# Moving the stationary operands of a two-layer decoder trunk to multiples of 512 bytes in SBUF

## The chip, the cores and the metric

The kernel runs on one core of one Trainium2 chip. The metric is the device time of one execution in microseconds (us). TensorE (PE in the profile) multiplies: it loads a stationary operand of up to 128 columns (LDWEIGHTS, shown as PEld) and then streams a moving operand of up to 512 columns past it. VectorE (DVE), ScalarE (ACT) and GpSimd (POOL) work on SBUF; SyncE (SP) issues the DMAs.

## The reference

Two layers over x (256 tokens, 1024 wide), all in float32:

```python
h = rmsnorm(x, g_mix);  proj = h @ w_in            # 1024 -> 7244 columns
A = stick_breaking_attention(qa, ka, va)           # 8 heads of 64
B = forgetting_attention(qb, kb, vb, log_f)        # 8 heads of 64
C = indexed_sparse_attention(qc, kc, vc, ...)      # top 64 keys, 2 kv heads
y = sum_b sigmoid(gate_b) * (branch_b @ w_branch[b])
x = x + y @ w_out
x = x + relu(rmsnorm(x, g_mlp) @ w_up)**2 @ w_down # 1024 -> 4096 -> 1024
```

After both layers a last RMSNorm with g_final gives the output. The weights are 149 MB, each read once.

## The kernel before, in words

Every product is made of three: both operands are split into a high part (float32r) and a rest, and `mm3` (L124 to L128) multiplies high by high (L126), high by low and low by high (L127, L128). Weights come by DMA on SP's queue into `raw` (four buffers); ACT makes the high part `whi` (L92), DVE the rest `wlo` (L93), four buffers each.

A matmul is written `pe.matmul(out, stationary, moving)`. The profile and the order of instructions write it the other way round, out<-moving,stationary: `mm<-whi,uh 128x512` streams 512 columns of `whi` past a stationary block of 128 columns of `uh`, and `mm<-xTh,whi 128x256` streams the 256 tokens of `xTh` past a stationary block of `whi`.

Products come in two manners. With weights stationary and 256 tokens moving: the q and k projections (`feat`), the gates, the branches (moving operand `k2h`, `k2l`) and w_up. With activations stationary and up to 512 weight columns moving (`stream_groups` and `stream_tok`, L198 to L219): the columns of attention C, the values (stationary `xTh`, `xTl`), w_out (stationary `yT`) and w_down (stationary `uh`, `ul`). In w_down the stationary operand changes with every matmul except between L126 and L127, which share `uh`.

Attention goes by pairs of heads. q is stationary (`qs`), k moves (L351, L352); the probabilities are transposed by TensorE, where the probabilities `e` or `R` are stationary and `ident` moves (L442); then v (`v` or `vc`) is stationary and the transposed probabilities `pTh`, `pTl` move (L458). Stick-breaking attention (L609 to L630) does the following for each of its four pairs of heads in each layer: ACT writes `th` = tanh(z/2) (L615), POOL masks it in place (two AFFINE_SELECTs, L618) and makes `m` = 0.5 - 0.5 th (L620), DVE runs a scan over `m` backwards (L626) and multiplies by 1 + th (L627). The scan takes `m` one element late, so `m` has 769 elements and three memsets:

```python
m = work.tile([128, 769], F32, name="m", tag="w3", bufs=4)
pool.tensor_scalar(m[:, 0:768], th..., -0.5, 0.5, ...)        # L620
pool.memset(m2[:, :, 0:1], 0.0)                               # L622
pool.memset(m2[:, :, 128:129], 0.0)                           # L623
pool.memset(m[:, 768:769], 0.0)                               # L624
dve.tensor_tensor_scan(R[:, ::-1], m[:, 1:769][:, ::-1], ...) # L626
```

SBUF is given out by pools that lie behind one another: `const`, `wp` (raw, whi, wlo), `t2` (xTh, xTl), `small`, and behind `small` either the layer's attention pool or, in the same place, its MLP pool (`uh`, `ul`). Within a pool tiles follow one another, each rounded up to 32 bytes; tiles of one tag share buffers of the largest one's size. So the size of every tile sets where those behind it lie. The order of work on each engine is set by a scheduler when the program is built.

Of the kernel before, what the change touches and what calls it, by code (L numbers as in the profile page):

```python
# [9 lines left out]
F32 = mybir.dt.float32  # L10
# [3 lines left out]
OP = mybir.AluOpType  # L14

T, D, DEPTH, COLS, DFF = 256, 1024, 2, 7244, 4096
NH, DH, BW, TOPK = 8, 64, 512, 64
FL0 = 3072
C0, CN = 3072, 1100
# [8 lines left out]
def AP(src, off, dims):  # L28
    return bass.AP(tensor=src.tensor, offset=src.offset + off, ap=[list(d) for d in dims])
# [3 lines left out]
def trunk_kernel(ctx: ExitStack, tc: tile.TileContext, x, positions, g_mix, w_in, b_forget, w_branch,  # L33
                 w_out, g_mlp, w_up, w_down, g_final, out):
    nc = tc.nc
    act, dve, pool, pe, dma = nc.scalar, nc.vector, nc.gpsimd, nc.tensor, nc.sync

    const = ctx.enter_context(tc.tile_pool(name="const", bufs=1))
    wp = ctx.enter_context(tc.tile_pool(name="wp", bufs=3))
    tp2 = ctx.enter_context(tc.tile_pool(name="t2", bufs=1))  # L40
    small = ctx.enter_context(tc.tile_pool(name="small", bufs=4))
# [5 lines left out]
    def at_tile(name="at"):  # L47
        return ps.tile([128, 512], F32, name=name, tag="at", bufs=2)
# [7 lines left out]

    xh = [const.tile([128, 2, 512], F32, name=f"x{h}") for h in range(2)]
    xs = [[xh[h][:, j, :] for h in range(2)] for j in range(2)]
    gload = const.tile([16, 128], F32, name="gload")
    gload2 = const.tile([16, 128], F32, name="gload2")  # L60

    def load_x(h):
        dma.dma_start(xh[h], AP(x, h * 512, [[D, 128], [128 * D, 2], [1, 512]]))
# [72 lines left out]
    def blk(tiles, k, c0=0, c1=256, p0=0, p1=128):  # L136
        h, l = tiles[k // 2]
        return h[p0:p1, k % 2, c0:c1], l[p0:p1, k % 2, c0:c1]
# [82 lines left out]
    att = None  # L221
    for layer in range(DEPTH):
# [8 lines left out]
        with tc.tile_pool(name=f"att{layer}", bufs=1, reuse_waits="tile") as att:  # L231
            work = att

            rp = at_tile("rp")
            for j in range(2):
                pe.transpose(rp[:, j * 128:j * 128 + 128], rstd[:, j:j + 1].to_broadcast([128, 128]), ident)
            rb = small.tile([128, 256], F32, name="rb", tag="rb", bufs=1)
            act.activation(rb, rp[:, 0:256], AF.Copy)


            ct = att.tile([128, 2, CN], F32, name="ct", tag="G", bufs=1)
            def ct_done(c0, n, o):
                for j in range(2):
                    act.activation(ct[:, j, c0:c0 + n], o[j][:, :n], AF.Copy, scale=rstd[:, j:j + 1])
# [4 lines left out]
            ct_done(368, 368, stream_tok(xt, 8, w_in, wi0 + C0 + 368, COLS, 368))  # L249

            if layer == 0:
                dma.dma_start(gload2, AP(g_mlp, 0, [[128, 16], [1, 128]]))
                pos = const.tile([128, 2], I32, name="pos")
                dma.dma_start(pos, AP(positions, 0, [[1, 128], [128, 2]]))
# [14 lines left out]
                ends = const.tile([128, 768], mybir.dt.bfloat16, name="ends")  # L269
# [6 lines left out]
                for q in range(2):  # L276
                    dve.tensor_scalar(self_[32 * q:32 * q + 8, :], ident[32 * q:32 * q + 8, 32 * q:32 * q + 8], -1.0, None,
                                      op0=OP.mult)
# [60 lines left out]
            for n, c in enumerate((KI, KC, KC + 64)):  # L339
# [3 lines left out]
                p = at_tile("kT")  # L343
# [15 lines left out]
            for j, c, n in SEG:  # L359
                for h in range(4):  # L360
                    z = at_tile("zi")
                    i = h % 2
# [5 lines left out]
                                             op0=OP.mult, op1=OP.add)  # L368

            for j, c, n in SEG:  # L370
                s = sc[:, c:c + n]
# [47 lines left out]
            p = at_tile("cum")  # L419
# [10 lines left out]
            p = at_tile("cumt")  # L430
            pe.matmul(p[:, 0:8], tri[:, 0:128], lf[:, 0, 0:8], start=True, stop=True)
            pe.matmul(p[:, 8:16], tri[:, 128:256], lf[:, 0, 0:8], start=True, stop=False)
            pe.matmul(p[:, 8:16], tri[:, 0:128], lf[:, 1, 0:8], start=False, stop=True)
            ctok = att.tile([128, 2, NH], F32, name="ctok")
            dve.tensor_copy(ctok, p[:, 0:16].rearrange("p (j h) -> p j h", j=2))


            def p_parts(e, i, scale):

                p = pt_tile("pT")  # L440
                for q in range(3):
                    pe.transpose(p[:, q * 128:q * 128 + 128], e[:, i, q * 128:q * 128 + 128], ident)  # L442
                hi = work.tile([128, 384], F32R, name="pTh", tag="pTh", bufs=2)
                lo = work.tile([128, 384], F32R, name="pTl", tag="pTl", bufs=2)
                act.activation(hi, p[:, 0:384], AF.Copy, scale=scale)
                dve.scalar_tensor_tensor(lo, p[:, 0:384], scale, hi.bitcast(F32), op0=OP.mult, op1=OP.subtract)
                return hi, lo

            def av_pair(parts, vwin, dst):


                o = av_tile()
                for i in range(2):
                    c = i * 256
                    for s, a, b, c0 in ((0, 0, 256, 0), (1, 256, 384, 128)):
                        v = vwin(i, s)
                        for n, p in enumerate(parts[i]):
                            pe.matmul(o[:, c + c0:c + 256], v, p[:, a:b], start=s == 0 and n == 0,  # L458
                                      stop=s == 1 and n == 1)
                hi, lo = dst  # L460
                t = work.tile([128, 256], F32, name="avs", tag="avs", bufs=2)
                for i in range(2):
                    act.activation(t[half(i)], o[half(1 - i), i * 256:i * 256 + 256], AF.Copy)
                for i in range(2):
                    dve.tensor_add(t[half(i)], o[half(i), i * 256:i * 256 + 256], t[half(i)])
                act.activation(hi, t, AF.Copy)
                dve.tensor_sub(lo, t, hi.bitcast(F32))
# [58 lines left out]
            def qk(z, qs, ks, b, i, opened=False):  # L526
                q, (kt, lo) = qs[b // 2], ks[b // 2]
                for j, c, n in SEG:
                    qk2(z[:, c:c + n], q[:, b % 2, i, j * 128:j * 128 + 128], kt[:, b % 2, i, 0:n],
                        lo[:, b % 2, i, 0:n], not opened, j == 1 or not opened)  # L530
# [79 lines left out]
            for b in range(4):  # L610
                th = work.tile([128, 2, 384], F32, name="th", tag="w3", bufs=4)
                for i in range(2):
                    z = at_tile("za")
                    qk(z, qa, ka, b, i)
                    act.activation(th[:, i, :], z[:, 0:384], AF.Tanh, scale=0.5)  # L615
                for c in (0, 256):
                    v = th[:, :, c:c + 128]
                    pool.affine_select(v, v, [[0, 2], [-1, 128]], OP.is_gt, -1.0, base=0, channel_multiplier=1)  # L618
                m = work.tile([128, 769], F32, name="m", tag="w3", bufs=4)
                pool.tensor_scalar(m[:, 0:768], th.rearrange("p i s -> p (i s)"), -0.5, 0.5, op0=OP.mult, op1=OP.add)  # L620
                m2 = m[:, 0:768].rearrange("p (i s) -> p i s", i=2)
                pool.memset(m2[:, :, 0:1], 0.0)  # L622
                pool.memset(m2[:, :, 128:129], 0.0)  # L623
                pool.memset(m[:, 768:769], 0.0)  # L624
                R = work.tile([128, 768], F32, name="R", tag="w3", bufs=4)
                dve.tensor_tensor_scan(R[:, ::-1], m[:, 1:769][:, ::-1], ends[:, ::-1], 0.0, op0=OP.mult, op1=OP.add)  # L626
                dve.scalar_tensor_tensor(R, th.rearrange("p i s -> p (i s)"), 1.0, R, op0=OP.add, op1=OP.mult)  # L627
                Rv = R.rearrange("p (i s) -> p i s", i=2)
                parts = [p_parts(Rv, i, 0.5) for i in range(2)]
                av_pair(parts, lambda i, s: va[:, s, 2 * b + i, :], blk(brA, b))  # L630
# [124 lines left out]
```

## Time and profile before

| | |
|---|---|
| median of 3 runs | 902.84 us (901.21 to 903.78) |
| the profiled execution's own time | 900.61 us |
| span of the profiled execution, first to last instruction | 898.6 us |
| granted TensorE clock, mean | 0.997 |
| PE busy | 882.3 us (98%) |
| DVE, ACT, POOL busy | 640.2 us, 530.2 us, 115.2 us |

PE's busy time counts matmuls whose ends are modelled and overlap, so it does not tell how fast TensorE works. That is read from the starts: the distance between the starts of successive matmuls is what each of them costs the stream. The timeline prints the start of each.

### The profile page before, as it was taken

Reading aid. Unit: us, or ns where it says so; the run is one execution under the profiler, and the core shown is the slowest. Engines: PE = TensorE matmul, PEld = TensorE weight load, DVE = VectorE, ACT = ScalarE, POOL = GpSimd, SP = SyncE. Lnnn points to the kernel's source line nnn. Section 1 sums busy time; section 2 is a strip of 40 time slices with the busy share of each in tenths; the row PEclk is TensorE's granted clock in tenths of the full one; section 3 lists DMA queues with packets and bytes.
Section 4 is the critical chain, followed back from the end, with each engine's and each line's share of the span. In section 5 each row is a group of like instructions: output and inputs, shape, how many; then the busy total and the mean of one; then the engine's idle time right before and its main releaser. Section 6 shows DMA issues by size and latency. Waiting matters only on the chain.

```text
span 898.6 us, 15648 instructions
## 1 busy us (share of the span) xinstructions
PE 882.3 (98%) x6174; PEld 828.8 (92%) x6174; DVE 640.2 (71%) x1032; ACT 530.2 (59%) x874; POOL 115.2 (13%) x222
## 2 busy tenths in 40 slices
PE   7999999999999999999999999999999999999996
PEld 7999999999989999888899999999999999998884
DVE  6889878997766666445468998799967666664542
ACT  6766876785465555434366759587744665553432
POOL 2300403352000000000011004043500100000001
PEclk9999999999999999999999999999999999999998
DMA  8746454244565554555466373543455565555521
GB/s 299 232 141 188 146 172 152 95 141 144 186 188 188 186 182 176 185 187 172 143 195 213 114 225 104 168 158 95 141 187 179 174 195 185 185 187 187 187 94 47
DMA packets 114777, 151.08 MB, mean 168 GB/s; under 512 B 2928, under 2 KB 82832, under 8 KB 114704
## 3 DMA queue, kind: packets, MB, share of 16 engines
q1 hardware_dynamic: 114704, 150.08, 51.2%
q8 instruction: 49, 0.80, 0.3%
q14 instruction: 24, 0.20, 0.1%
HBM read 149.02 MB, written 1.05 MB: 167 GB/s over the span
## 4 chain that ended last, share of the span: by engine, by line
PE 91%; DVE 4%; POOL 2%; issue 2%; DMA 1%; SPq 0%; ACT 0%; POOLq 0%; DVEq 0%; ACTq 0%
PE mm L128 26%; PE mm L126 26%; PE mm L127 26%; PE av L458 2%; PE at L128 1%; PE at L127 1%; PE at L126 1%; PE pT L442 1%; DVE R L626 1%; POOL m L620 1%; PE xtp L175 1%; DVE ksl L160 1%; DMA x<-in_x_dram 1%; POOL th L618 1%; DVE wlo L93 1%
## 5 line engine op out<-in xcount | busy, mean ns | idle before, releaser
L93 DVE TENSOR_TENSOR wlo<-raw,whi 128x1024 fp32r<-128x1024 f32 (+3 forms) x289 | 349.8, 1213 | 192.5 <-ACT whi L92 191.4
L92 ACT ACTIVATE whi<-raw 128x1024 fp32r<-128x1024 f32 (+3 forms) x289 | 298.6, 1035 | 278.8 <-PE mm L127 142.2
L126 PE MATMUL mm<-xTh,whi 128*128 128x256 f32 x1136 | 322.7, 284 | 0.0
L128 PE MATMUL mm<-xTh,wlo 128*128 128x256 f32 x1136 | 322.2, 284 | 0.0
L127 PE MATMUL mm<-xTl,whi 128*128 128x256 f32 x1136 | 322.0, 283 | 0.0
L126 PEld LDWEIGHTS mm<-xTh,whi 128*128 128x128 f32 x1136 | 217.6, 192 | 0.3
L127 PEld LDWEIGHTS mm<-xTl,whi 128*128 128x128 f32 x1136 | 217.6, 192 | 0.2
L128 PEld LDWEIGHTS mm<-xTh,wlo 128*128 128x128 f32 x1136 | 217.6, 192 | 0.1
L128 PE MATMUL mm<-whi,ul 128*128 128x512 f32 x256 | 101.6, 397 | 0.0
L127 PE MATMUL mm<-wlo,uh 128*128 128x512 f32 x256 | 101.5, 396 | 0.0
L126 PE MATMUL mm<-whi,uh 128*128 128x512 f32 x256 | 101.1, 397 | 0.0
L192 POOL TENSOR_TENSOR ms<-ss 128x2 f32<-128x2 f32 (+1 forms) x6 | 4.3, 719 | 481.1 <-ACT junk L185 301.6
L128 PEld LDWEIGHTS mm<-whi,ul 128*128 128x128 f32 x256 | 48.2, 188 | 11.7
L127 PEld LDWEIGHTS mm<-wlo,uh 128*128 128x128 f32 x256 | 48.2, 188 | 11.6
L126 PEld LDWEIGHTS mm<-whi,uh 128*128 128x128 f32 x256 | 48.2, 188 | 11.6
L128 PE MATMUL mm<-k2h,wlo 128*128 128x256 f32 x192 | 54.1, 284 | 0.0
L126 PE MATMUL mm<-k2h,whi 128*128 128x256 f32 x192 | 53.6, 284 | 0.0
L127 PE MATMUL mm<-k2l,whi 128*128 128x256 f32 x192 | 53.6, 282 | 0.0
L127 PE MATMUL mm<-wlo,xTh 128*128 128x512 f32 (+2 forms) x128 | 46.3, 363 | 0.0
L126 PE MATMUL mm<-whi,xTh 128*128 128x512 f32 (+2 forms) x128 | 46.1, 365 | 0.1
L128 PE MATMUL mm<-whi,xTl 128*128 128x512 f32 (+2 forms) x128 | 45.7, 363 | 0.0
L491 POOL TENSOR_SCALAR e<-e,rs 128x128 f32<-128x128 f32 x64 | 34.4, 556 | 16.6 <-DVE rs L488 16.4
(214 smaller groups left out, 1306.4 us busy)
## 6 DMA issues: line engine op xcount, KB each, us to landing
raw<-in_w_in_dram SPq DMA_DIRECT2D x48, 1024.0 KB, 5.0
raw<-in_w_up_dram SPq DMA_DIRECT2D x32, 1024.0 KB, 5.3
raw<-in_w_down_dram SPq DMA_DIRECT2D x32, 1024.0 KB, 4.9
raw<-in_w_branch_dram SPq DMA_DIRECT2D x12, 1024.0 KB, 4.9
raw<-in_w_out_dram SPq DMA_DIRECT2D x8, 1024.0 KB, 5.0
raw<-in_w_in_dram SPq DMA_DIRECT2D x8, 736.0 KB, 5.8
raw<-in_w_in_dram SPq DMA_DIRECT2D x3, 728.0 KB, 4.4
out_dram<-x SPq DMA_DIRECT2D x4, 256.0 KB, 2.4
```

Source lines behind the costliest of these rows:

```text
L92: act.activation(h3[:, i:i + m], raw[:, i:i + m], AF.Copy)
L93: dve.tensor_sub(l3[:, i:i + m], raw[:, i:i + m], h3[:, i:i + m].bitcast(F32))
L126: pe.matmul(o, ah, bh, start=start, stop=False)
L127: pe.matmul(o, ah, bl, start=False, stop=False)
L128: pe.matmul(o, al, bh, start=False, stop=stop)
L160: dve.tensor_sub(lo[half(i), :, i, :], src[half(i)], dst[half(i), :, i, :].bitcast(F32))
L175: pe.transpose(p[:, i * 256 + j * 128:i * 256 + j * 128 + 128], xs[j][h][:, c:c + 128], ident)
L442: pe.transpose(p[:, q * 128:q * 128 + 128], e[:, i, q * 128:q * 128 + 128], ident)
L458: pe.matmul(o[:, c + c0:c + 256], v, p[:, a:b], start=s == 0 and n == 0, stop=s == 1 and n == 1)
L491: pool.tensor_scalar(e[:, i, c:c + n], e[:, i, c:c + n], rs[:, i, j:j + 1], 1.0, op0=OP.mult, op1=OP.mult)
L618: pool.affine_select(v, v, [[0, 2], [-1, 128]], OP.is_gt, -1.0, base=0, channel_multiplier=1)
L620: pool.tensor_scalar(m[:, 0:768], th.rearrange("p i s -> p (i s)"), -0.5, 0.5, op0=OP.mult, op1=OP.add)
```

## The change

Tiles get other sizes or other pools, so that the tiles behind them lie elsewhere: `gload2` takes the buffer of `gload` (512 bytes less in `const`), `rb` is padded from 256 to 280 floats and `ctok` (64 bytes) moves into `small` (160 bytes more there, so that the pools behind it start at byte 119,808, which is 234 times 512, where they started at 120,160); `ct` is padded from 1100 to 1152 columns; `m` shrinks from 769 to 768 elements, so that the buffers of its tag are 3072 bytes apart where they were 3104. For that `m` is written one element earlier from `th` taken one element later, which leaves out one of its three memsets.

```diff
-    gload = const.tile([16, 128], F32, name="gload")
-    gload2 = const.tile([16, 128], F32, name="gload2")
+    gload = const.tile([16, 128], F32, name="gload", tag="gload")
...
-            rb = small.tile([128, 256], F32, name="rb", tag="rb", bufs=1)
+            rb = small.tile([128, 280], F32, name="rb", tag="rb", bufs=1)[:, 0:256]
...
-            ct = att.tile([128, 2, CN], F32, name="ct", tag="G", bufs=1)
+            ct = att.tile([128, 2, 1152], F32, name="ct", tag="G", bufs=1)[:, :, 0:CN]
...
             if layer == 0:
+                gload2 = const.tile([16, 128], F32, name="gload2", tag="gload")
                 dma.dma_start(gload2, AP(g_mlp, 0, [[128, 16], [1, 128]]))
...
-            ctok = att.tile([128, 2, NH], F32, name="ctok")
+            ctok = small.tile([128, 2, NH], F32, name="ctok", tag="ctok", bufs=1)
...
-                m = work.tile([128, 769], F32, name="m", tag="w3", bufs=4)
-                pool.tensor_scalar(m[:, 0:768], th.rearrange("p i s -> p (i s)"), -0.5, 0.5, op0=OP.mult, op1=OP.add)
-                m2 = m[:, 0:768].rearrange("p (i s) -> p i s", i=2)
-                pool.memset(m2[:, :, 0:1], 0.0)
-                pool.memset(m2[:, :, 128:129], 0.0)
-                pool.memset(m[:, 768:769], 0.0)
+                m = work.tile([128, 768], F32, name="m", tag="w3", bufs=4)
+                pool.tensor_scalar(m[:, 0:767], th.rearrange("p i s -> p (i s)")[:, 1:768], -0.5, 0.5,
+                                   op0=OP.mult, op1=OP.add)
+                m2 = m.rearrange("p (i s) -> p i s", i=2)
+                pool.memset(m2[:, :, 127:128], 0.0)
+                pool.memset(m2[:, :, 383:384], 0.0)
                 R = work.tile([128, 768], F32, name="R", tag="w3", bufs=4)
-                dve.tensor_tensor_scan(R[:, ::-1], m[:, 1:769][:, ::-1], ends[:, ::-1], 0.0, op0=OP.mult, op1=OP.add)
+                dve.tensor_tensor_scan(R[:, ::-1], m[:, ::-1], ends[:, ::-1], 0.0, op0=OP.mult, op1=OP.add)
```

What that does to the addresses in the two built programs (bytes past the last multiple of 512; matmuls of both layers):

| stationary operand | matmuls | moving operand, columns | stationary starts at, before | after | moving starts at, before | after |
|---|---|---|---|---|---|---|
| `uh`, `ul` (w_down) | 768 | whi, wlo, 512 | 352 | 0 | 0 | 0 |
| `yT` (w_out) | 192 | whi, wlo, 512 | 448 | 0 | 0 | 0 |
| `xTh`, `xTl` (values) | 192 | whi, wlo, 512 | 0 | 0 | 0 | 0 |
| `xTh`, `xTl` (columns of C) | 288 | whi, wlo, 364 or 368 | 0 | 0 | 0 or more | the same |
| `whi`, `wlo` (feat, gates, w_up) | 3456 | xTh, xTl, 256 | 0 | 0 | 0 | 0 |
| `whi`, `wlo` (branches) | 576 | k2h, k2l, 256 | 0 | 0 | 128 | 0 |
| `qs` | 224 | ks, ksl, kh, kl, 128 and 256 | 448 | 0 | 448 | 0 |
| `v` | 128 | pTh, pTl, 128 and 256 | 128 | 0 | 128 | 0 |
| `vc` | 64 | pTh, pTl, 128 and 256 | 64 or 320 | 0 or 256 | 128 | 0 |
| `e`, `R` (transposes) | 144 | ident, 128 | 0, 32, 448, 480 | 0 | 128 | 128 |
| `x` (transposes) | 64 | ident, 128 | 128 | 128 | 128 | 128 |

The rest (`ct`, `kdup`, `lf`, `tri`, `sel`, `rstd`, `gload`) is 68 matmuls; of these `kdup` comes to 0 and the others stay off a multiple of 512.

PE, DVE and ACT execute the same instructions in the same order as before. POOL's order changes in stick-breaking attention; this is what stood there before, from the mask of the first pair to that of the second, with the tiles' numbers (m_1938 and th_1919 belong to the first pair, m_1997 and th_1978 to the second):

```order
L618 AFFINE_SELECT th_1919<-th_1919 128x2x128
L620 TENSOR_SCALAR m_1938<-th_1919 128x768 [waits DVE_49,Pool_49]
L624 MEMSET m_1938 128x1
L622 MEMSET m_1938 128x2 [waits Pool_49]
L623 MEMSET m_1938 128x2
L624 MEMSET m_1997 128x1 [waits DVE_49]
L618 AFFINE_SELECT th_1978<-th_1978 128x2x128 [waits Activation_49,Pool_49]
L618 AFFINE_SELECT th_1978<-th_1978 128x2x128
L620 TENSOR_SCALAR m_1997<-th_1978 128x768 [waits Pool_49]
```

And this is the same stretch in the changed program (m_1996 and th_1977 belong to the second pair there):

```order
L618 AFFINE_SELECT th_1919<-th_1919 128x2x128
L621 TENSOR_SCALAR m_1938<-th_1919 128x767 [waits DVE_49,Pool_49]
L624 MEMSET m_1938 128x2 [waits Pool_49]
L625 MEMSET m_1938 128x2
L618 AFFINE_SELECT th_1977<-th_1977 128x2x128 [waits DVE_49,Activation_49]
L618 AFFINE_SELECT th_1977<-th_1977 128x2x128
L621 TENSOR_SCALAR m_1996<-th_1977 128x767 [waits DVE_49,Pool_49]
```

The one-element memset of the second pair's `m`, which stood ahead of that pair's mask and waited for DVE's multiplication L627 of the first pair, is gone. The mask now waits for the first pair's scan, which comes before L627 on DVE, and `m` itself waits for L627.

On SP's queue nothing moves, but the load of `gload2` (the row of L252) now waits for TensorE as well, since its buffer is the one that the transpose of `gload` reads. Before:

```order
L105 DMA raw_269<-in_w_in_dram 128x4x368 [waits DMAHW2_49]
L252 DMA gload2_73<-in_g_mlp_dram 16x128 [waits DMAHW3_49]
L254 DMA pos_378<-in_positions_dram 128x2x1 [waits DMAHW4_49]
```

And in the changed program:

```order
L104 DMA raw_268<-in_w_in_dram 128x4x368 [waits DMAHW2_49]
L252 DMA gload2_376<-in_g_mlp_dram 16x128 [waits DMAHW3_49,PE_49]
L254 DMA pos_378<-in_positions_dram 128x2x1 [waits DMAHW4_49]
```

Behind that row stand the loads of positions and of b_forget and then all later weights.

## Rows read from the trace of the kernel before

**Rows 1.** The page: busy time by engine, granted clock by slice of the span.

```profile
PE 882.3 (98%) x6174; PEld 828.8 (92%) x6174; DVE 640.2 (71%) x1032; ACT 530.2 (59%) x874; POOL 115.2 (13%) x222
...
PEclk9999999999999999999999999999999999999998
```

**Rows 2.** Timeline of PE in w_down, layer 0: start us, us, instruction.

```profile
364.74 0.40 PE L128 MATMUL mm<-whi,ul 128*128 128x512 f32 x1
...
405.98 0.39 PE L127 MATMUL mm<-wlo,uh 128*128 128x512 f32 x1
```

**Rows 3.** Timeline of PE in the values of layer 1.

```profile
586.82 0.39 PE L128 MATMUL mm<-whi,xTl 128*128 128x512 f32 x1
...
592.26 0.39 PE L128 MATMUL mm<-whi,xTl 128*128 128x512 f32 x1
```

**Rows 4.** Timeline of PE in w_out, layer 0.

```profile
245.76 0.39 PE L127 MATMUL mm<-wlo,yT 128*128 128x512 f32 x1
...
259.96 0.39 PE L126 MATMUL at<-whi,yT 128*128 128x512 f32 x1
```

**Rows 5.** Stretches: width, busy us of PE, PEld, DVE, ACT, POOL (instructions), clock, DMA.

```profile
365.00:405.00 40.00, 40.00 (x172) 32.19 (x171) 18.40 (x17) 15.32 (x15) 0.00 (x0) 1.00 0.55 191
587.00:592.00 5.00, 5.00 (x23) 4.14 (x23) 4.83 (x5) 4.80 (x8) 0.95 (x6) 1.00 0.68 210
```

**Rows 6.** Groups by line and form: the count of w_down's, w_out's and the branches' matmuls.

```profile
L128 PE MATMUL mm<-whi,ul 128*128 128x512 f32 x256 | 101.6, 397 | 0.0
...
L128 PE MATMUL mm<-k2h,wlo 128*128 128x256 f32 x192 | 54.1, 284 | 0.0
...
L128 PE MATMUL mm<-whi,yT 128*128 128x512 f32 x32 | 12.6, 394 | 0.0
```

**Rows 7.** Timeline of PE, 256 columns moving: in a branch, then in w_up.

```profile
232.07 0.28 PE L126 MATMUL mm<-k2h,whi 128*128 128x256 f32 x1
...
243.34 0.28 PE L128 MATMUL mm<-k2h,wlo 128*128 128x256 f32 x1
...
299.84 0.28 PE L128 MATMUL mm<-xTh,wlo 128*128 128x256 f32 x1
...
300.92 0.28 PE L128 MATMUL mm<-xTh,wlo 128*128 128x256 f32 x1
```

**Rows 8.** Timeline of PE in attention: scores, then values of attention C.

```profile
168.30 0.22 PE L351 MATMUL zb<-ks,qs 128*128 128x128 f32 x1
...
168.76 0.28 PE L127 MATMUL mm<-xTl,whi 128*128 128x256 f32 x1
...
564.49 0.33 PE L458 MATMUL av<-pTh,vc 128*128 128x256 f32 x1
...
564.95 0.30 PE L442 MATMUL pT<-ident,e 128*128 128x128 f32 x1
```

**Rows 9.** The chain that ended last: start us, us on the chain, what.

```profile
109.87 0.68 PE pT L442 x6
```

**Rows 10.** Timeline of POOL, ACT, DVE, PE in stick-breaking, layer 0 (idle before <-releaser).

```profile
150.41 0.10 POOL L624 MEMSET m<- 128x1 f32 x1 [3.97 <-DVE R L627]
...
149.39 0.88 ACT L615 ACTIVATE th<-za 128x384 f32<-128x384 f32 x2
...
155.10 1.76 DVE L626 TENSOR_TENSOR_SCAN R<-m,ends 128x768 f32<-128x768 f32 x1 [0.53 <-POOL m L623]
...
173.59 0.36 PE L458 MATMUL av<-pTh,v 128*128 128x256 f32 x1 [0.85 <-DVE avs L465]
```

**Rows 11.** The tile `m`: durations ns min/median/max, first and last start; who waited (us, times).

```profile
L620 POOL TENSOR_SCALAR m<-th x8: 1557/1735/1865, 144.5 to 607.1; 128x768 f32<-128x768 f32 x8
...
  DVE R L626: 1.1, 2
```

**Rows 12.** Timeline of SP and PE at the start.

```profile
6.20 2.45 SPq L252 DMA_DIRECT2D gload<-in_g_mlp_dram  x1
...
5.03 0.25 PE L77 MATMUL gps<-ident,gload 16*128 16x16 f32 x1 [5.03 <-DMA gload<-in_g_mix_dram]
```

## The prediction

> **What bounds the kernel now.** I read the page first. TensorE is busy nearly the whole span and its granted clock is full in every slice but the last [rows 1], which is the level of 2.4 GHz, and little time is lost to waits. What can still be gained lies in how close the matmuls follow one another, and busy time does not show that: one 512-column matmul is listed at some 397 ns [rows 6], but its neighbours start sooner. So I took the distance between starts from the timeline, over long undisturbed stretches, and compared stretches that differ in the stationary operand.
>
> The comparison that decides is between w_down and the values of attention. Both come from the same function, with 512 columns of `whi` or `wlo` moving from the same buffers (offset 0 past a multiple of 512 bytes), the same order of the three products and two PSUM tiles in turn. In w_down, 176 distances lie between 364.74 and 405.98 [rows 2]: 41.24 / 176 = 0.2343 us each. In the values, 24 lie between 586.82 and 592.26 [rows 3]: 5.44 / 24 = 0.2267 us. The stationary operand starts at 352 in the first and at 0 in the second. w_out has `yT` at 448: 62 distances between 245.76 and 259.96 [rows 4], 14.20 / 62 = 0.2290 us. So the same matmul costs 226.7, 229.0 or 234.3 ns for offsets 0, 448 and 352.
>
> Could something else make w_down slow? I looked at the stretches [rows 5]: the clock is 1.00 in both, PE has no gap, and the dearer stretch is the one with less beside it: DVE 18.40 of 40 us against 4.83 of 5, DMA share 0.55 against 0.68. Load from other engines would order them the other way. Distance in memory is no better: `yT` lies in the same region as `uh`, and is cheap. What is left among the differences I can see is the start of the stationary block.
>
> **The change part by part.**
>
> *w_down.* `uh` and `ul` go to 0. There are 768 such matmuls: three groups of 256, of which [rows 6] show one. 768 x (0.2343 - 0.2267) = 5.8 us less. They follow one another without a wait, so all of it is on the path: the end of w_down is the end of the kernel but for the last normalisation. The Trainium skill, in "TensorE: Matmul & The Clock Gate", section "LDWEIGHTS (loading the stationary operand)", makes the load of a stationary block a matter of its number of columns alone. By that rule the start would not count and this term would be 0; the three distances above, with 128 stationary columns in each, do not agree with it. I go by the rows.
>
> *w_out.* 192 matmuls, six groups of 32 like the one in [rows 6]: 192 x (0.2290 - 0.2267) = 0.4 us less.
>
> *Branches.* Here the stationary weights lay at 0 already, and it is the moving operand that goes from 128 to 0. 95 distances between 232.07 and 243.34 [rows 7] make 0.1186 us each. With both operands at 0 the same form takes, in w_up, 9 distances from 299.84 to 300.92 [rows 7], 0.1200 us. So this part gets a little worse: 576 matmuls (three groups of 192 [rows 6]) x 0.0014 = 0.8 us more. At the other end it does not move at all, 0.
>
> *Attention's products.* `qs`, `v` and `vc` are stationary in 416 matmuls of 128 and 256 columns, in fours. The last four of a score take 168.76 - 168.30 = 0.46 us (`qs` at 448), four of the values of C 564.95 - 564.49 = 0.46 us (`vc` at 64 or 320) [rows 8]: two quite different offsets, one price. No row has such a four at 0. Bounds: six transposes, each of which also changes its stationary block, take 0.68 us [rows 9], 0.113 each, so a four at that price takes 0.45; with 0.120 apiece, as where both operands are at 0 [rows 7], it takes 0.48. Over 104 fours that is from 1.0 us less to 2.1 us more. I take 0, since the two offsets that were measured cost the same.
>
> *Transposes.* `e` and `R` go to 0 from four different offsets. They cost 0.113 us apiece in the six of [rows 9]; 144 of them between that and the 0.120 of two operands at 0 is 0 to 1.0 us more. I take 0. The 64 transposes of `x` keep their offset of 128.
>
> *POOL in stick-breaking.* Eight one-element memsets of 0.10 us go [rows 10], all off PE's path. The order changes at the second pair: the mask no longer stands behind the memset that waited for L627 until 150.41. But the mask needs `th`, which ACT finishes at 149.39 + 0.88 = 150.27 [rows 10], so it starts at most some 0.3 us sooner, and `m` waits for L627 in any case. DVE's scan had waited 0.53 us for this `m`, twice in all [rows 10, 11], and a DVE that is late there is what PE waits for at 173.59 [rows 10]. So between 0.6 us less over both layers and, if masks that run earlier get into DVE's way, as much more. I take 0.
>
> *The load of `gload2`.* It waits for the transpose of `gload` now. That one ended at 5.03 + 0.25 = 5.28, and SP came to the load at 6.20 [rows 12]: nothing behind it is delayed. If the transpose slipped past 6.20, everything behind it on SP would be late by as much; the first weights stand ahead of it.
>
> *The sum.* -5.8 - 0.4 + 0.8 = -5.4 us. Against the profiled execution of 900.6 us that is 895.2; it lay 2.2 us below the median of the three runs, so for the median 902.84 - 5.4 = 897.4 us.
>
> **The rivals.** A measurement of this kernel can tell about 0.3% (2.7 us) from no change, so 900.1 and 905.5 are the limits below.
>
> *First: the start has no part in it, and w_down is slower for a reason that I do not see* (for instance that `uh` and `ul` are many tiles of which each is used once in a pass). Then nothing moves but small terms: 902.8 us. For it speaks that both offsets are even multiples of 32 bytes, and that a transpose at any of its offsets costs the same; against it that w_out, which also goes through its tiles once, costs 229 ns and not 234. The Trainium skill ("SBUF — State Buffer", section "Specifications (TRN2)") gives lines of 16 bytes in which an operand should be read; 352 and 448 are whole numbers of such lines, so by it the blocks were aligned already and this rival holds. The three distances speak against that.
>
> *Second: the gain comes, but attention pays for it*, because streams whose two operands start at the same offset cost 0.120 us per matmul even where they were cheaper. This is the upper bound of the two attention terms together: -5.4 + 2.1 + 1.0 = -2.3, or 900.5 us. For it speaks the branches' step from 0.1186 to 0.1200; against it that `qs` and `ks` both lay at 448 already, and their fours cost what those of `vc` against `pTh` cost.
>
> *Third, slower: POOL reads `th` one element past its start.* If such a read is slow on POOL, `m` (1.735 us in the middle [rows 11]) becomes the bound of stick-breaking attention. It is made eight times, and the scan waits for it with no slack in two of them [rows 11]; at most the others pass their delay on as well. If each of the eight were late by d, the kernel would lose 8 d. To end above 905.5 it must lose 8.1 us with the gain of 5.4 standing, so d = 1.0 us and `m` 2.7 us or more; at twice its time, d = 1.7, it would be 902.8 - 5.4 + 13.9 = 911.3 us. For it: POOL is slow per element here, so a less convenient read could show. Against it: the start of a row moves by one float, and the number of elements read stays; and DVE's scan, which so far read `m` from its second element, does so at its usual length in [rows 10].
>
> That the change does not do what it says can be seen in the addresses: some operands stay off 512. They are transposes of x and a few dozen small matmuls, and I have put nothing down for them.
>
> **How the numbers follow.** My forecast, 897.4 us, has a chance of 0.84. The first rival has 0.08, the second 0.05, the third 0.03. Around the forecast the open terms give from -1.0 - 0.6 - 0.8 = 2.4 less to some 3 more at their ends, which will not all come at once, and three runs before spread over 2.6 us; so 894.0 to 900.5 us, which takes in the second rival and leaves out the first and third. Faster by over 0.3%: the forecast and half of the second rival's scatter about its limit, 0.86. Within 0.3%: the first rival and the other half, 0.11. Slower: 0.03.
>
> **What would show it.** In the changed profile the distance between starts in w_down should be 0.2267 us where it was 0.2343, in w_out 0.2267 where it was 0.2290, in the branches 0.1200; w_up and the values stay. The two w_down stages should end 2.9 us sooner each. A four in attention should stay at 0.46, `m` at some 1.7 us, and PE's wait at the place of 173.59 the same within half a microsecond. If w_down stays at 0.2343 I am wrong altogether; if it goes to 0.2267 and the time does not fall by 5 us, look for the loss in attention.

## The result, and the profile after

The changed kernel takes 897.51 us (median of 6 runs, 895.16 to 898.94) where the kernel before takes 902.59 (6 runs, 901.21 to 904.19) beside it: a ratio of 0.994 [0.9924, 0.9957], or 5.1 us less. The profiled execution took 897.73 us, with a span of 895.7. The forecast was 897.4 us in 894.0 to 900.5. The number was right. What the prediction named as its cause was only partly right, and the experiments are mostly about that.

The page says little, as in [rows 1]: TensorE is busy for the same share of the span, and its granted clock is full but for the last slice and, as the fourth experiment will show, the first microseconds. One group shows the gain and one shows that most is unchanged; compare the mean ns of one with [rows 6]. The first two fences are the page of the changed kernel: busy time with the clock by slices, then groups.

```profile
PE 879.0 (98%) x6174; PEld 830.7 (93%) x6174; DVE 640.5 (72%) x1032; ACT 530.0 (59%) x874; POOL 115.0 (13%) x214
...
PEclk9999999999999999999999999999999999999998
```

```profile
L127 PE MATMUL mm<-whi,ul 128*128 128x512 f32 x256 | 99.7, 389 | 0.0
...
L127 PE MATMUL mm<-k2h,wlo 128*128 128x256 f32 x192 | 54.3, 285 | 0.0
```

w_down's matmul went from 397 to 389 ns, the branch's from 284 to 285. These are listed durations, which overlap; the time lies in the distances between starts. The timeline of PE in the changed kernel, first w_down of layer 0, then w_out of layer 0, then a branch, then the place of the wait of 173.59 in [rows 10]:

```profile
365.80 0.39 PE L125 MATMUL mm<-whi,uh 128*128 128x512 f32 x1
...
405.92 0.39 PE L125 MATMUL mm<-whi,uh 128*128 128x512 f32 x1
```

```profile
247.82 0.39 PE L127 MATMUL mm<-whi,yT 128*128 128x512 f32 x1
...
262.11 0.39 PE L127 MATMUL mm<-whi,yT 128*128 128x512 f32 x1
```

```profile
234.46 0.28 PE L125 MATMUL mm<-k2h,whi 128*128 128x256 f32 x1
...
245.86 0.28 PE L127 MATMUL mm<-k2h,wlo 128*128 128x256 f32 x1
```

```profile
175.78 0.36 PE L458 MATMUL av<-pTh,v 128*128 128x256 f32 x1 [0.85 <-DVE avs L465]
```

In w_down 177 distances make 40.12 us, 0.2267 each, where [rows 2] gave 0.2343. In w_out 63 make 14.29 us, 0.2268, where [rows 4] gave 0.2290. In the branch 95 make 11.40 us, 0.1200, where [rows 7] gave 0.1186. And PE waits for DVE at the same place for the same 0.85 us. The two fours of attention of [rows 8] take 0.46 us in the changed kernel too, and the values stay at 0.2267. So these readings came out as the prediction said.

POOL's `m` and DVE's wait for it stand as they were in [rows 11]. The view of the tile `m` in the changed kernel (duration in ns: least, median, most; then, under who waited for it, DVE's scan):

```profile
L621 POOL TENSOR_SCALAR m<-th x8: 1568/1752/1885, 146.6 to 606.9; 128x767 f32<-128x767 f32 x8
...
  DVE R L627: 1.1, 2
```

Making `m` takes 1752 ns against 1735, and the scan waits for it twice, 1.1 us in all, as before. The eight memsets that went left nothing in these waits.

The gain can be placed with four starts. The same four instructions, start of w_down in layer 0, first matmul of layer 1, start of w_down in layer 1, last matmul; in the kernel before, then in the changed one (timeline of PE):

```profile
359.36 0.39 PE L126 MATMUL mm<-whi,uh 128*128 128x512 f32 x1
...
450.18 0.33 PE L126 MATMUL mm<-whi,xTh 128*128 128x364 f32 x1
...
800.16 0.39 PE L126 MATMUL mm<-whi,uh 128*128 128x512 f32 x1
...
889.88 0.40 PE L128 MATMUL mm<-whi,ul 128*128 128x512 f32 x1
```

```profile
361.69 0.40 PE L125 MATMUL mm<-whi,uh 128*128 128x512 f32 x1
...
449.73 0.33 PE L125 MATMUL mm<-whi,xTh 128*128 128x364 f32 x1
...
800.09 0.40 PE L125 MATMUL mm<-whi,uh 128*128 128x512 f32 x1
...
886.93 0.39 PE L127 MATMUL mm<-whi,ul 128*128 128x512 f32 x1
```

w_down falls from 90.82 to 88.04 us in layer 0 and from 89.72 to 86.84 in layer 1, so by 2.8 and 2.9 us. The rest of layer 1 grows from 349.98 to 350.36. But the changed kernel is already 2.33 us late when it comes to its first w_down, so this one profile ends only 2.95 us sooner. Where that lateness comes from is the fourth experiment's question.

### The profile page after: what moved, and what is told of

Its sections match the earlier page's. It is cut to its first block, busy times and chain, and to the rows that moved or that the text cites. A ratio compares the mean times of both kernels' runs of the same rounds, so it can differ in the third digit from the quotient of the medians.

```text
span 895.7 us, 15647 instructions
## 1 busy us (share of the span) xinstructions
PE 879.0 (98%) x6174; PEld 830.7 (93%) x6174; DVE 640.5 (72%) x1032; ACT 530.0 (59%) x874; POOL 115.0 (13%) x214
## 4 chain that ended last, share of the span: by engine, by line
PE 90%; DVE 5%; issue 1%; POOL 1%; ACT 1%; DMA 1%; SPq 0%; POOLq 0%; DVEq 0%; ACTq 0%
PE mm L125 26%; PE mm L126 26%; PE mm L127 26%; PE av L458 2%; DVE R L627 2%; PE at L126 1%; PE at L127 1%; PE at L125 1%; PE pT L442 1%; PE xtp L174 1%; DVE wlo L92 1%; DMA x<-in_x_dram 1%; DVE qs L151 0%; PE zc L352 0%; PE zc L351 0%
## 5 line engine op out<-in xcount | busy, mean ns | idle before, releaser
L127 PE MATMUL mm<-whi,ul 128*128 128x512 f32 x256 | 99.7, 389 | 0.0
L126 PE MATMUL mm<-wlo,uh 128*128 128x512 f32 x256 | 99.6, 389 | 0.0
L125 PE MATMUL mm<-whi,uh 128*128 128x512 f32 x256 | 99.2, 389 | 0.0
L126 PEld LDWEIGHTS mm<-k2l,whi 128*128 128x128 f32 x192 | 36.7, 192 | 0.0
```

The source lines that it names most:

```text
L125: pe.matmul(o, ah, bh, start=start, stop=False)
L126: pe.matmul(o, ah, bl, start=False, stop=False)
L127: pe.matmul(o, al, bh, start=False, stop=stop)
```

## The experiments

Unless another base is named, an edit is made to the changed kernel. A start is given in bytes past a multiple of 512. Every kernel computes all that the kernel before does.

**Is it w_down alone?** `down_only` is the kernel before with one more allocation. It brings `uh` and `ul` to 0 and leaves every other operand where it was.

```diff
             uT = []
+            mlp.tile([128, 40], F32, name="pad")
```

> The kernel before with one part of the change alone: 160 unused bytes ahead of uh and ul put them at 0 past a multiple of 512 where they were at 352; nothing else moves. Theory (the start of the stationary block sets the distance between matmuls): the distance in w_down falls from 0.2343 to 0.2267 us, 768 x 7.6 ns = 5.8 us less, ratio 0.9936; w_out stays at 0.2290 and the branches at 0.1187. Rival (w_down is slower for another reason): 0.2343 stays, ratio 1.000.

It took 897.54 us (5 runs), a ratio of 0.9947 [0.9933, 0.996]. One unused allocation of 160 bytes in a partition gives the whole gain.

**And the other way round?** `down_back` takes the changed kernel and puts `uh` and `ul` back at 352.

```diff
             uT = []
+            mlp.tile([128, 88], F32, name="pad")
```

> The changed kernel with 352 unused bytes ahead of uh and ul: they are back at 352, all else as changed. Theory: w_down back at 0.2343, 5.8 us more than the changed kernel; against the kernel before what is left of the change is w_out (-0.4), the branches (+0.6 to +0.8) and attention (about +0.6 by the starts of the matmuls in the changed kernel's trace), so 0.4 to 1.0 us slower than before, ratio 1.000 to 1.001. Rival: w_down stays at 0.2267, ratio 0.994.

It took 903.1 us (11 runs), a ratio of 1.0003 [0.9992, 1.0013]. All that the change does beside w_down, the other operands, the memsets and the new pools, is too small for the times to show; the traces put it at 0.8 us more, as the end of the fourth experiment shows. The timeline of PE in w_down of layer 0, first of `down_only`, then of `down_back`:

```profile
365.71 0.39 PE L127 MATMUL mm<-wlo,uh 128*128 128x512 f32 x1
...
403.79 0.39 PE L127 MATMUL mm<-wlo,uh 128*128 128x512 f32 x1
```

```profile
365.61 0.40 PE L127 MATMUL mm<-whi,ul 128*128 128x512 f32 x1
...
403.80 0.39 PE L125 MATMUL mm<-whi,uh 128*128 128x512 f32 x1
```

168 distances in 38.08 us, 0.2267; 163 in 38.19 us, 0.2343.

**A repeat.** `after_again` is the changed kernel, unedited, beside the two above.

> The changed kernel once more, for a narrower interval and a second look at its start. In its first profile the 150th matmul began 1.9 us later than in the profile of the kernel before, with some of the first transposes 0.213 us apart. If that belongs to the change (the load of gload2 that now waits for TensorE, or another order of transfers), the start is late again and the time is 897.5. If it is chance, the start differs from the first profile's by one or two us, and the times spread over 3 us or more as before. Ratio 0.993 to 0.995 by either.

898.6 us (5 runs), 0.9952 [0.9939, 0.9965]. It agrees with the first measurement, and with `down_only` within the intervals. Its trace is late at the start too (the 151st matmul at 34.63 us), which does not yet tell the change from chance; the next run does.

**Where do the 1.9 us at the start come from?** In the first profile the changed kernel reaches the same early matmul, the 151st, 1.95 us later than the kernel before (33.99 against 32.04). `before_again` is the kernel before, unedited, profiled a second time.

> The kernel before once more, for a second profile of its start. If the late start is the change's, the 150th matmul begins at 32.0 us again, to within 0.3. If it is chance, it can begin 1 to 2 us later. The distances in w_down are 0.2343 either way.

It took 903.28 us in one run, and its 151st matmul starts at 34.75 us: the kernel before can be as late as the changed one. So the late start is chance and no part of the change, and the first profile of before was a lucky one. The view of the tile `xtp` shows where the time goes (ns: least, median, most; first and last start), for the kernel before, for it again, and for the changed kernel:

```profile
L175 PE MATMUL xtp<-ident,x x8: 272/272/332, 10.0 to 10.8; 128*128 128x128 f32 x8
```

```profile
L175 PE MATMUL xtp<-ident,x x8: 421/421/476, 10.5 to 12.0; 128*128 128x128 f32 x8
```

```profile
L174 PE MATMUL xtp<-ident,x x8: 421/421/474, 10.6 to 12.1; 128*128 128x128 f32 x8
```

The second set of eight transposes of `x` takes 272 or 421 ns apiece, and their starts lie 109 or 213 ns apart, in the same kernel, from one execution to the next. The cause is TensorE's clock. Each trace records when a level of it was granted, and the first record says 1.00, full speed (2.4 GHz). That record begins at 8.78 us in the kernel before, earlier than these eight, and at 15.33 us in `before_again` and 13.51 us in the changed kernel, later than these eight. Earlier than that nothing is recorded, and the 1.00 that the views print there stands on no record. The pace shows the level: the timeline of PE in `before_again`, columns of attention C, around 15.33 us:

```profile
14.97 0.50 PE L126 MATMUL mm<-whi,xTh 128*128 128x364 f32 x1
15.27 0.36 PE L127 MATMUL mm<-wlo,xTh 128*128 128x364 f32 x1
15.47 0.33 PE L128 MATMUL mm<-whi,xTl 128*128 128x364 f32 x1
15.64 0.33 PE L126 MATMUL mm<-whi,xTh 128*128 128x364 f32 x1
```

The same form comes every 0.30 us up to there and every 0.17 us from there on. In all twelve traces the pace rises within one matmul of the first record. In `before` and `down_back` the record begins before the eight transposes (8.78 and 7.67 us) and they take 272 ns; in the other ten it begins after them (12.87 to 16.12 us) and they take 417 or 421. So until the record begins TensorE ran at the lower level (1.2 GHz). Why it rises sooner in one execution than in another stays open; the two profiles of the kernel before show that the change does not decide it.

With the start set aside, the traces tell much more than the times. The first line of each pair is the 151st matmul, the second the last one; the kernel before again, `down_only`, `down_back`, then the 151st of the kernel before and of the changed kernel, whose last ones stand above:

```profile
34.75 0.33 PE L128 MATMUL mm<-whi,xTl 128*128 128x368 f32 x1
892.57 0.40 PE L128 MATMUL mm<-whi,ul 128*128 128x512 f32 x1
```

```profile
33.37 0.33 PE L128 MATMUL mm<-whi,xTl 128*128 128x368 f32 x1
885.51 0.39 PE L128 MATMUL mm<-whi,ul 128*128 128x512 f32 x1
```

```profile
31.80 0.33 PE L127 MATMUL mm<-whi,xTl 128*128 128x368 f32 x1
890.47 0.40 PE L127 MATMUL mm<-whi,ul 128*128 128x512 f32 x1
```

```profile
32.04 0.33 PE L128 MATMUL mm<-whi,xTl 128*128 128x368 f32 x1
```

```profile
33.99 0.33 PE L127 MATMUL mm<-whi,xTl 128*128 128x368 f32 x1
```

The kernel before takes 857.84 us from one to the other, and 857.82 again; the changed kernel 852.94, and 852.97 in `after_again`. Two traces of one kernel agree to 0.03 us. So the change gains 4.9 us; `down_only` (852.14) gains 5.7, where 5.8 was forecast for w_down; and `down_back` (858.67) loses 0.8. The rest of the change does cost something, and the one allocation alone is better than the change by that much, though their times do not tell them apart.

**Which starts are cheap?** `curve32` moves `uh` and `ul` on by 32 bytes after every second tile, so that w_down goes through all 16 multiples of 32.

```diff
+                if c % 2 == 0 and c + layer > 0:
+                    mlp.tile([128, 64 if c == 0 else 8], F32, name=f"pad{c}")
```

> The changed kernel with small gaps between the uh and ul tiles, so that w_down goes through sixteen starts past a multiple of 512: 0, 32, 64 to 224 in layer 0 and 256 to 480 in layer 1, 48 matmuls of each. Theory: the distance depends on the start; 0 gives 0.2267, 352 0.2343, 448 0.2290. If any start off 512 costs, all but 0 lie above 0.2267; if a finer step decides (64 or 128 bytes), the starts fall into two or three prices by that step. Rival (the number of tiles or their order decides): all sixteen alike.

It took 901.13 us in one run. The timeline of PE in w_down of layer 1, every 24th matmul, where the start moves from 256 on by 32 each time:

```profile
801.49 0.40 PE L125 MATMUL mm<-whi,uh 128*128 128x512 f32 x1
...
806.97 0.39 PE L125 MATMUL mm<-whi,uh 128*128 128x512 f32 x1
...
812.56 0.40 PE L125 MATMUL mm<-whi,uh 128*128 128x512 f32 x1
...
834.97 0.40 PE L125 MATMUL mm<-whi,uh 128*128 128x512 f32 x1
...
840.48 0.40 PE L125 MATMUL mm<-whi,uh 128*128 128x512 f32 x1
...
846.07 0.39 PE L125 MATMUL mm<-whi,uh 128*128 128x512 f32 x1
```

At 256, 5.48 us for 24 (228 ns, settling at 226.7); at 288, 5.59 (233); at 448, 5.51 (229.6); at 480, 5.59 again. Over both layers: 0 and 256 settle at 226.7, 192 and 448 make 229.4, and the other twelve 232.8 to 233.7 (means without the distances in which PE waits, as all means by difference below). So the pattern repeats every 256 bytes, not every 512, and the 229 ns of w_out in [rows 4] was the price of 448, which is 192 modulo 256.

**The start, or the distance to the other operand?** In all of this the moving operand began at 0, so a start and a difference of two starts were the same thing. `whi352` puts `whi` and `wlo` at 352, `xT` at 0, and `uh` at 0 in layer 0 and at 352 in layer 1.

```diff
...
+        if not padded:
+            padded.append(wp.tile([128, 88], F32, name="wpad", tag="wpad", bufs=1))
...
+            if layer == 1:
+                mlp.tile([128, 88], F32, name="pad")
...
-            ct = att.tile([128, 2, 1152], F32, name="ct", tag="G", bufs=1)[:, :, 0:CN]
+            ct = att.tile([128, 2, CN], F32, name="ct", tag="G", bufs=1)
```

> The changed kernel with whi and wlo at 352 past a multiple of 512, xT at 0 as before, uh and ul at 0 in layer 0 and at 352 in layer 1 (attention's tiles come to 96). In w_down whi and wlo move, in w_up they are stationary. Theory (the start of the stationary block alone counts): w_down 0.2267 in layer 0 and 0.2343 in layer 1; w_up, now stationary at 352, above 0.120. Rival (the distance between the two starts counts, both at the same offset being cheap): w_down dearer than 0.2267 in layer 0 and 0.2267 in layer 1. Second rival (the moving start counts alike): dearer in both layers.

The timeline of PE in `whi352`: w_up (`xT` at 0 moving, `whi` at 352 stationary), w_down of layer 0 (`uh` at 0 against 352), w_down of layer 1 (352 against 352):

```profile
299.78 0.28 PE L131 MATMUL mm<-xTh,wlo 128*128 128x256 f32 x1
...
319.97 0.28 PE L129 MATMUL mm<-xTh,whi 128*128 128x256 f32 x1
...
369.65 0.39 PE L131 MATMUL mm<-whi,ul 128*128 128x512 f32 x1
...
399.99 0.40 PE L129 MATMUL mm<-whi,uh 128*128 128x512 f32 x1
...
809.80 0.39 PE L130 MATMUL mm<-wlo,uh 128*128 128x512 f32 x1
...
848.79 0.39 PE L131 MATMUL mm<-whi,ul 128*128 128x512 f32 x1
```

Layer 0, with every stationary block at 0: 130 distances in 30.34 us, 0.2334, the dear price. Layer 1, with every stationary block at 352: 172 in 38.99 us, 0.2267, the cheap one. The absolute start is refuted; what counts is where the stationary block begins relative to the moving operand, modulo 256 bytes. Of the multiples of 32, zero is best for 512 columns. For 256 columns it is not: w_up, now 96 apart, makes 172 distances in 20.19 us, 0.1174, where it made 0.1200 at zero. There are some 3,450 matmuls of that kind against 768 in w_down, and so this kernel, with half of w_down at the dear price, took 892.93 us in one run, less than the changed one.

The Trainium skill ("TensorE: Matmul & The Clock Gate", section "Step-by-step: what each phase is for") gives the load of the next stationary block a read port of its own, so that it takes no read bandwidth from the matmul that runs. By that rule the distance between the two starts should not matter; layers 0 and 1 of `whi352`, 0.2334 and 0.2267, do not agree with it. That it is these two reads that meet is not shown by any run.

**Two ways to use it.** `xT128` moves only `xT`, to 128, and leaves w_down at zero apart. (In this and in `apart64`, `rb` is also cut and `r2` gets a single buffer, which sets where the pools behind them start.)

```diff
...
+        if not padded and tag == "xT":
+            padded.append(tp2.tile([128, 32], F32, name="tpad", tag="tpad", bufs=1))
...
```

> The changed kernel with xT at 128 where it was at 0, all other operands unmoved. xT moves past whi and wlo in 3456 matmuls of 256 columns. In the kernel before the branches ran at 0.1187 with k2 moving at 128, and at 0.1200 in the changed kernel with k2 at 0. If the moving start does that, w_up and the projections go to 0.1187: 3456 x 1.3 ns = 4.5 us less than the changed kernel, ratio 0.989 against the kernel before. If it belonged to the branches alone, 0.1200 stays and the ratio is 0.994 to 0.995. Where xT is stationary (480 matmuls of 364 to 512 columns) the start at 128 should cost 0 to 7.6 ns each, up to 3.6 us more.

It took 894.17 us (5 runs), 0.9917 [0.9903, 0.9931]. The 256-column streams take 118.7 ns at 128 apart, and the values, whose stationary block is now the one at 128, 232.4 in place of 228.2. `curve256` sets the four buffers of `whi`, and those of `wlo`, 0, 32, 64 and 96 bytes from `xT`, for the curve of 256 columns; `k2` lies at 128:

```diff
...
+                for b in range(4):
+                    if p + b:
+                        wp.tile([128, 8 if b else 40], F32, name=f"gap{p}{b}", tag=f"gap{p}{b}", bufs=1)
+                    first.append(wp.tile([128, 1024], F32R, name=w, tag=f"{w}{b}", bufs=1))
...
+            att.tile([128, 8], F32, name="gapk")
```

> The changed kernel with the four buffers of whi and of wlo at 0, 32, 64 and 96 past a multiple of 256 bytes, xT at 0 and k2 at 128, so that the products with 256 moving columns go through eight differences between the start of the stationary and of the moving operand: 0 to 96 in the projections, gates and w_up, 128 to 224 in the branches. New theory (the difference of the two starts modulo 256 bytes sets the distance): 0 gives 0.1200, 96 some 0.1175 as with whi at 352, 128 some 0.1187 to 0.1195 as with k2 or xT at 128, and the best of them lies below 0.1200, so that a layout with a difference of 0 is the best for 512 moving columns and the worst for 256. If the old theory (the start of the stationary block alone) held here, 0 would be the cheapest or all alike. The time itself tells nothing: w_down runs at four differences at once.

896.02 us in one run. Means in ns by difference: 0 119.5, 32 118.3, 64 117.1, 96 118.1, 128 119.1, 160 119.5, 192 117.8, 224 117.4. The spread is smaller than in w_down and the order another; at 64 the distances fell to 113 to 114 after some ten matmuls of a stretch. A difference does not set the pace at once: w_down changes its own every 12 matmuls here, and at 0 it takes a mean of 230.1 and reaches 226.6 only in the last three of the twelve. So `apart64` puts `whi` and `wlo` 64 bytes past `xT` and `k2`, and `uh` and `yT` at 64 too, so that they stay zero apart from `whi`:

```diff
...
+        if not padded:
+            padded.append(wp.tile([128, 16], F32, name="wpad", tag="wpad", bufs=1))
...
+        if len(padded) == 1 and tag == "xT":
+            padded.append(tp2.tile([128, 48], F32, name="tpad", tag="tpad", bufs=1))
...
+            att.tile([128, 48], F32, name="kpad")
...
```

> The changed kernel with whi, wlo, uh, ul and yT at 64 past a multiple of 256 bytes and xT and k2 at 0: the difference of the starts is 0 for w_down and w_out and 64 for all products with 256 moving columns; xT as stationary comes to a difference of 192. By the new theory (the difference modulo 256 decides; in the trace of the run with eight differences the stretches at 64 settled at 0.1133 us after some ten matmuls, where 0 has 0.1200): 4032 x 6.7 ns = 27 us less than the changed kernel, w_down and w_out unmoved, xT stationary 192 x 2.3 ns and as much for 288 shorter ones, 1 us more; 871 us, ratio 0.965 to 0.970, if DVE and ACT keep up. If 64 holds only as the mean over those short stretches, 0.1171, it is 4032 x 2.9 = 12 us: 887 us, ratio 0.983. If the old theory holds (the stationary start at a multiple of 512 is the cheapest), w_down goes to 0.2333 and the time lies above the changed kernel's, ratio 1.000 or more.

It took 882.02 us (5 runs, 881.85 to 885.39): 0.9782 [0.9761, 0.9803] of the kernel before, 20 us less, and the fastest here. The timeline of PE in `apart64`, a stretch of gates and a branch of layer 0, then w_up:

```profile
224.74 0.28 PE L130 MATMUL mm<-xTl,whi 128*128 128x256 f32 x1
...
235.96 0.28 PE L130 MATMUL mm<-k2l,whi 128*128 128x256 f32 x1
...
299.80 0.28 PE L129 MATMUL mm<-xTh,whi 128*128 128x256 f32 x1
...
319.94 0.28 PE L129 MATMUL mm<-xTh,whi 128*128 128x256 f32 x1
```

99 distances in 11.22 us, 0.1133, in the first; 171 in 20.14 us, 0.1178, in the second. Both stretches have the same forms and the same difference of 64, and each keeps its pace to its end: the time lies between the two that were expected because some stretches run at one pace and some at the other. It is not mere chance, since w_up runs at 117.8 in both layers, and the gates and the last branch before it at 113.3 in both. What puts a stretch into one of them stays open. Summed over the trace, the 256-column streams of `xT` and `k2` take 14.2 us less than in the changed kernel (475.99 against 490.15).

**Finer than 32 bytes.** `fine` sets the buffers of `whi` at 16, 48, 80 and 112, and those of `wlo` at 144, 176, 208 and 240.

```diff
-        hi = wp.tile([128, 1024], F32R, name="whi", tag="whi", bufs=4)
-        lo = wp.tile([128, 1024], F32R, name="wlo", tag="wlo", bufs=4)
+        hi = wp.tile([128, 1032], F32R, name="whi", tag="whi", bufs=4)[:, 4:1028]
+        lo = wp.tile([128, 1032], F32R, name="wlo", tag="wlo", bufs=4)[:, 4:1028]
...
```

> Here whi begins 16, 48, 80 and 112 bytes past a multiple of 256, wlo 144, 176, 208 and 240; xT and uh stay at 0. Theory (the difference of the two starts modulo 256 bytes sets the spacing, and it changes gradually around 64): 256-column matmuls with a difference of 48 and 80 come at 113 to 118 ns, those with 16 and 112 at 118 to 120; w_down, whose spacing is low only at differences of 0 and 192, stays at 233 to 234 ns for all eight. First rival (what counts is the 32-byte unit in which a start falls): 16 is like 0 and 48 like 32, so w_down with 16 takes 226.7 to 229 ns and the 256-column matmuls take those of the start rounded down. Second rival (only whole multiples of 32 bytes run at full rate): every 256-column spacing is over 120 ns. Time by the theory: between 900 and 904 us, w_down as in the kernel before and the 256-column streams up to 1.5 ns shorter.

894.68 us in one run, and no theory was right. w_down comes at 228.2 to 232.4 ns at these differences, between its cheap and its dear price, where 233 to 234 was expected, and the 256-column streams at 116 to 120, with 48 at 119.8 no better than the rest. Here the difference changes from one matmul to the next, since `whi` and `wlo` alternate, and the run does not separate that from the finer step.

## Why the prediction was right, and where it was not

The terms, each against the sum of all distances from a start to the next in the two profiles, in us:

| term | predicted | before | after | measured |
|---|---|---|---|---|
| w_down, 768 matmuls | -5.8 | 179.84 | 174.17 | -5.67 |
| w_out, 192 | -0.4 | 44.15 | 43.81 | -0.34 |
| branches, 576 | +0.8 | 69.47 | 70.04 | +0.57 |
| attention's products, 416 | 0 (-1.0 to +2.1) | 47.16 | 47.51 | +0.35 |
| transposes of `e` and `R`, 144 | 0 (0 to +1.0) | 12.82 | 12.85 | +0.03 |
| POOL, DVE's scan | 0 (-0.6 to +0.6) | | | wait unchanged |
| sum | -5.4 | | | -5.06 by the terms, -5.1 by the medians |

With the 256-column products whose operands do not move (+0.16) the terms make the 4.9 us that the traces show from the 151st matmul on.

**The sizes** held because the rows for them came from the same kind of stream. The branches' +0.8 was taken from one stretch at 0.1186; over all 576, the starts of runs among them, it was 0.1206 before and 0.1216 after, and the step is 0.0010 where 0.0014 was put down. Attention came out at a sixth of its upper end: its fours do get dearer, by 3 ns each (0.35 / 104) and not by 20. The second rival's reason, two operands with the same start, does not explain it: `qs` and `v` had that before as well (448 and 448, 128 and 128 in the table of the change) and still cost 0.17 and 0.09 more; `vc`, which goes from 192 apart to 0, costs 0.11 more. In the two traces of each kernel these sums agree to 0.02, so the rise is real, and its cause stays open.

**The step that failed** is "What is left among the differences I can see is the start of the stationary block". In each of [rows 2 to 4] the moving operand began at 0, so the start and the distance between the two starts were one number, and I took the simpler. `whi352` separates them and decides for the distance. The step was enough for this change, because it also leaves the moving operands of w_down and w_out at 0, and the number came out; as far as the cause goes, that is luck. As a rule for the next change it would have been wrong twice: multiples of 256 do as well as those of 512, and aligning all operands alike brings the 256-column matmuls, the larger part of this kernel, to a difference as dear as any measured (119.5 ns at 0 and at 160 in `curve256`). The evidence was in the rows: the branches' moving operand at 128 was cheaper than at 0 [rows 7], which a rule on stationary starts does not say, and the prediction used that price without asking why. A smaller misreading: the prediction calls the clock full in every slice but the last, and the first slice is not, since the record begins at 8.78 us and TensorE ran at half pace ahead of it.

**The first rival** (the start has no part in it) falls with `down_only`: nothing but the start of `uh` and `ul` moved there, and the time fell by 0.5%. **The third** (POOL slow on the shifted read) falls with the 1752 ns of `m` and with `down_back`, which keeps the shifted read and is within 0.8 us of the kernel before. The load of `gload2` held nothing up.

## What to carry to other kernels

Where matmuls follow one another without a wait, read the distance between their starts, not the listed duration, and compare it between streams of the same form; a few ns times some thousand matmuls is more than most waits. In this kernel one unused allocation of 160 bytes was worth 5 us, and a few that set the two operands 64 bytes apart in the 256-column streams 15 us more: so try the difference of the two starts, modulo 256 bytes, for each form of matmul by itself, and do not take "aligned" for "best". Compare two traces from a matmul that comes after the rise of the clock: here that told 0.8 us, where the times could not. When rows vary one thing, write down what else was constant in all of them, since a rule read from them may be about that.

## What the runs showed of the hardware that was not expected

- A stream of loads and matmuls whose granted clock is 1.00 and that waits for nothing has a pace that depends on the difference of the starts of its two operands: 226.7 ns at 0, 229 at 192, 232.4 to 234.3 at the other multiples of 32 for 512 columns; 119.5 to 120 at 0 and 117.1 to 119.5 elsewhere for 256 columns, with 113.3 in some stretches at 64. These are prices of long stretches; after a change of the difference it took some nine matmuls to reach 226.6. Why was not found; that two reads of the memory meet would fit, but was not shown.
- At a difference of 64 the same form runs at 113.3 ns in one stretch and 117.8 in another, and keeps it.
- The moment at which TensorE's clock comes to full speed differs by some 8 us between executions (the record begins at 7.67 to 16.12 us in the twelve traces), also in the same kernel (8.78 and 15.33), and moves the whole execution: the two profiles of the kernel before start their last matmul 2.69 us apart, and were 2.71 us apart at the 151st already. A single pair of profiles can be wrong by that much: this one showed 2.95 us of a gain of 5.1. From a matmul after the rise to the last one, two traces of one kernel agreed to 0.03 us.
